# Layer 0 of a two-layer hybrid stack: where the modulation weights are fetched from, and how many places the gated z rows have

## The chip, the core and the metric

The kernel runs on one core of one Trainium2 chip. Its time is the device time of one execution in microseconds (us), taken from the host side of the program; the profile gives one execution's span, from its first instruction to its last. Five engines run their own instruction lists in order and wait for each other by semaphores: TensorE (PE), VectorE (DVE), ScalarE (ACT), GpSimd (POOL) and SyncE (SP). DMAs are issued by an engine's list too, and wait in it like any other instruction.

## The reference, cut to what matters

The program computes two blocks for 1024 tokens of 1024 channels. The first block has two layers, both modulated: from a vector `c`, `silu(c) @ ada_w[l] + ada_b[l]` gives a shift, a scale and a gate of 1024 each. Layer 0, the only part that the change touches, is this:

```
h    = rmsnorm(x) * (1 + scale) + shift
proj = h @ in_w                        # x half and z half, 1024 each
xf   = causal conv of 4 taps (x half)
r, i = sigmoid(block-diagonal gates of xf)
a    = exp(-8 * r * softplus(-lambda));  b = sqrt(1 - a^2) * (i * xf)
hseq = scan of  h_t = a_t * h_(t-1) + b_t
y    = hseq * silu(z half)
x    = x + gate * (y @ out_w)
```

Layer 1 (a gated delta rule) and the second block (convolution and state space) follow; the modulation of layer 1 needs its own columns of `ada_w`, and some of these are summed during layer 0.

## The kernel before, in words

Weights come as fp32 tiles `wst` of 1 MB over SP's queue (`load_w`, L101), and are split in two fp16 parts by ACT (`wh`, L104) and DVE (`wl`, L105), with two `wst` places and four places for the parts. A projection of 128 channels by 512 tokens is 24 matmuls (L111 to L113) into one of three PSUM places (`ps_mm`), which ACT empties: as `xp` for the x half (L323), as `silu` into `zs` for the z half (L542).

Layer 0 runs over four pairs of channel blocks. `xbranch(p)` projects the x half, makes the convolution (one ACT pass L329 and three DVE passes L331 for each of two halves e = 0 and 1), the gates (`ps_gate` matmuls L512, which wait for the L331 passes of their half, and ACT sigmoids L513), then decay and input on ACT and DVE (L519 to L528) and the scan (L531). `zbranch(p)` projects the z half in four groups; each goes through ACT L542 into a `zs` tile, is multiplied by `hseq` on DVE (L543), and split in two fp16 parts (ACT L123, DVE L125). There are two `zs` places.

Beside this run six sums of modulation columns, each over four tiles `ast` of 512 KB (24 tiles in all, four places). `ada_fetch` issues the four DMAs of one sum (L161), `ada_sum` makes eight DVE passes over them (L148 for the first, L150 for seven more), `ada_fin` transposes the sum on PE (L185), reduces and adds it on DVE (L186, L187) and writes 512 numbers to DRAM from POOL's queue (`ada_d`, L189). Each of these writes is a [128 x 4] tile of single fp32 numbers that go to scattered places of 4 bytes. The sums are called 1 to 6 here, and the tiles 1 to 24.

The order of instructions on each engine is not the order of the code: a list scheduler of the tile framework makes it, from dependences, places and its own estimate of times. So a change of a queue or of a number of places also moves instructions on engines that the diff doesn't name. Before the change POOL's list in this stage has little in it: clearing three columns of each `xp` (L313), and the six `ada_d` writes.

Of the kernel before, what the change touches and what calls it, by code (L numbers as in the profile page):

```python
# [10 lines left out]
F32 = mybir.dt.float32  # L11
# [6 lines left out]
P = 128  # L18
# [10 lines left out]
def kernel(ctx, tc, ins, out):  # L29
    nc = tc.nc  # L30
    pe, dve, act, pool, sp = nc.tensor, nc.vector, nc.scalar, nc.gpsimd, nc.sync
    a = ins

    def mkpool(name, bufs=1, space=None, stack=ctx):
        kw = {} if space is None else {"space": space}
        if space is not DRAM:
            kw["reuse_waits"] = "tile"
        return stack.enter_context(tc.tile_pool(name=name, bufs=bufs, **kw))
# [7 lines left out]
    def ps_mm(n="psmm"):  # L46
        return psmm.tile([P, 512], F32, tag="mm", name=n, bufs=3)
# [60 lines left out]
    def mm_chT(ps, w, c0, ah, al, nk=NK, ks=None):  # L108
        wh, wl = w
        for k in (range(nk) if ks is None else ks):  # L110
            pe.matmul(ps, wh[:, k, c0:c0 + P], ah(k), start=(k == 0), stop=False)  # L111
            pe.matmul(ps, wh[:, k, c0:c0 + P], al(k), start=False, stop=False)  # L112
            pe.matmul(ps, wl[:, k, c0:c0 + P], ah(k), start=False, stop=(k == nk - 1))  # L113
# [8 lines left out]
    def split(h, l, src, scale=1.0):  # L122
        act.activation(h, src, AF.Copy, scale=scale)  # L123
        if scale == 1.0:
            dve.tensor_tensor(out=l, in0=src, in1=h, op=ALU.subtract)  # L125
        else:
            dve.scalar_tensor_tensor(out=l, in0=src, scalar=scale, in1=h, op0=ALU.mult, op1=ALU.subtract)
# [24 lines left out]
    def ada_src(l, part, h, k0, n):  # L152
        c0 = D * part + 512 * h
        return a["ada_w"][l, P * k0:P * (k0 + n), c0:c0 + 512].rearrange("(k p) c -> p k c", p=P)

    def ada_fetch(pl, l, part, h):

        tiles = []
        for kk in range(4):
            st = pl.tile([P, 2, 512], F32, tag="ast", name="ast", bufs=4)  # L160
            sp.dma_start(st, ada_src(l, part, h, 2 * kk, 2))  # L161
            tiles.append(st)
        return tiles, l, part, h

# [74 lines left out]
    def hTh(sl):  # L239
        t = hT["h"]  # L240
        return lambda k: t[:, k, sl]

    def hTl(sl):
        t = hT["l"]
        return lambda k: t[:, k, sl]
# [88 lines left out]
    def shift_proj(w):  # L334
        wh, wl = w
        ps = ps_s("ps_sh")
        for e in range(2):
            es = slice(P * e, P * (e + 1))
            for k in range(NK):
                pe.matmul(ps[:, 2 * e:2 * e + 2], wh[:, k, es], shl[:, k, :], start=(k == 0), stop=False)  # L340
                pe.matmul(ps[:, 2 * e:2 * e + 1], wl[:, k, es], shl[:, k, 0:1], start=False, stop=(k == NK - 1))
        r = gwp.tile([P, 2, 2], F32, tag="shr", name="shr", bufs=3)
        act.activation(r.rearrange("p e t -> p (e t)"), ps[:, 0:4], AF.Copy, scale=IWS)
        dve.tensor_tensor(out=r[:, :, 0], in0=r[:, :, 0], in1=r[:, :, 1], op=ALU.add)
        return [r[:, e, 0:1] for e in range(2)]

    with ExitStack() as s0:
        pl = mkpool("ln0", stack=s0)
# [123 lines left out]
    with ExitStack() as sy:  # L472
        ypool = mkpool("y0", stack=sy)
        yT = []
        with ExitStack() as s0:
            pl = mkpool("lru", stack=s0)
# [57 lines left out]
            def zbranch(p, w):  # L534
                sb = shift_proj(w)
                for e in range(2):
                    yT.append([])
                    for hf in range(2):
                        ps = ps_mm()
                        mm_chT(ps, w, P * e, hTh(HF[hf]), hTl(HF[hf]))  # L540
                        zs = pl.tile([P, 512], F32, tag="zs", name="zs", bufs=2)
                        act.activation(zs, ps, AF.Silu, scale=IWS, bias=sb[e])  # L542
                        dve.tensor_tensor(out=zs, in0=zs, in1=hseq[p][:, e, HF[hf]], op=ALU.mult)  # L543

                        y = hseq[p][:, e, HF[hf]].bitcast(F16)
                        yT[-1].append((y[:, :512], y[:, 512:]))
                        split(y[:, :512], y[:, 512:], zs)

            adq = [(l, part, h) for l, part in ((0, 2), (1, 1), (1, 0)) for h in range(2)]
            adt, adp = [ada_fetch(pl, *adq.pop(0))], []  # L550

            def ada_step():
                if len(adp) == 2 or not adt:
                    ada_fin(pl, *adp.pop(0))
                if adt:
                    adp.append(ada_sum(pl, *adt.pop(0)))
                if adq:
                    adt.append(ada_fetch(pl, *adq.pop(0)))
# [5 lines left out]
            ada_step()  # L564
            wx.append(load_w(a["lru_in_w"][0], 3 * WC))
            zbranch(0, wz[0])
            ada_step()
            xbranch(2, wx[2])
            wz.append(load_w(a["lru_in_w"][0], D + 2 * WC))
            ada_step()  # L570
            zbranch(1, wz[1])
            wz.append(load_w(a["lru_in_w"][0], D + 3 * WC))
            ada_step()
            ada_step()
            xbranch(3, wx[3])
            ada_step()
            ada_step()
            zbranch(2, wz[2])
            ada_step()
            zbranch(3, wz[3])  # L580
        with ExitStack() as s0:
            pl = mkpool("out0", stack=s0)
# [29 lines left out]
    with ExitStack() as s0:  # L612
        pl = mkpool("gdn", stack=s0)
# [349 lines left out]
    with ExitStack() as s0:  # L963
        pl = mkpool("out1", stack=s0)
# [588 lines left out]
```

## Time and profile before

| | us |
|---|---|
| median of three runs | 1833.15 |
| lowest and highest | 1831.11, 1836.46 |
| the profiled execution, its time | 1828.97 |
| the profiled execution, its span | 1827.3 |
| PE busy | 1741.6 (95%) |
| DVE busy | 1386.6 (76%) |
| ACT busy | 920.1 (50%) |
| POOL busy | 62.1 (3%) |

PE is busy nearly everywhere, so what a change is worth is read from the stretches where it is not. Times are counted from the start of the span. Layer 0's four pairs run from about 80 to 273 us; everything later has the same order of instructions before and after.

### The profile page before, as it was taken

Reading aid. Unit: us, or ns where it says so; the run is one execution under the profiler, and the core shown is the slowest. Engines: PE = TensorE matmul, PEld = TensorE weight load, DVE = VectorE, ACT = ScalarE, POOL = GpSimd, SP = SyncE. Lnnn points to the kernel's source line nnn. Section 1 sums busy time; section 2 is a strip of 40 time slices with the busy share of each in tenths; the row PEclk is TensorE's granted clock in tenths of the full one; section 3 lists DMA queues with packets and bytes.
Section 4 is the critical chain, followed back from the end, with each engine's and each line's share of the span. In section 5 each row is a group of like instructions: output and inputs, shape, how many; then the busy total and the mean of one; then the engine's idle time right before and its main releaser. Section 6 shows DMA issues by size and latency. Waiting matters only on the chain.

```text
span 1827.3 us, 28998 instructions
## 1 busy us (share of the span) xinstructions
PE 1741.6 (95%) x11591; PEld 1072.6 (59%) x11591; DVE 1386.6 (76%) x2429; ACT 920.1 (50%) x1642; POOL 62.1 (3%) x152
## 2 busy tenths in 40 slices
PE   4978999999899999999999998999999999999998
PEld 2433449855556656678789586555444444444487
DVE  6697767656777777887466799999999999693332
ACT  6576663256556857766443434655651221571221
POOL 0000000000000010100000300000000000000000
PEclk8999999999999999999999999999999999999999
DMA  9554345314142231444342311101321221011212
GB/s 305 164 157 140 57 72 190 104 55 132 30 120 69 62 79 33 113 130 117 128 150 82 89 50 52 53 20 51 127 81 35 70 69 64 30 41 52 81 70 93
DMA packets 165169, 165.23 MB, mean 90 GB/s; under 512 B 50094, under 2 KB 143342, under 8 KB 165034
## 3 DMA queue, kind: packets, MB, share of 16 engines
q1 hardware_dynamic: 163626, 159.17, 29.0%
q0 software_dynamic: 1408, 4.21, 0.6%
q8 instruction: 91, 1.49, 0.3%
q14 instruction: 44, 0.36, 0.1%
HBM read 139.05 MB, written 23.12 MB: 89 GB/s over the span
## 4 chain that ended last, share of the span: by engine, by line
PE 61%; DVE 25%; ACT 6%; issue 4%; DMA 3%; SPq 0%; DVEq 0%; ACTq 0%
DVE cc L1024 5%; PE psmm L113 5%; PE psmm L111 5%; PE psmm L112 5%; DVE wl L105 2%; PE ps_out L120 2%; PE ps_out L118 2%; PE ps_out L119 2%; PE ps_fin L120 2%; PE ps_fin L118 2%; PE ps_fin L119 2%; PE ps_zc L111 2%; PE ps_zc L113 2%; PE ps_zc L112 2%; ACT jk L728 1%
## 5 line engine op out<-in xcount | busy, mean ns | idle before, releaser
L111 PE MATMUL psmm<-hTh,wh 128*128 128x512 f16 x896 | 342.2, 383 | 12.7 <-ACT zs L542 10.2
L112 PE MATMUL psmm<-hTl,wh 128*128 128x512 f16 x896 | 342.8, 383 | 0.1
L113 PE MATMUL psmm<-hTh,wl 128*128 128x512 f16 x896 | 342.8, 383 | 0.0
L1024 DVE SCALAR_TENSOR_TENSOR cc<-cu,cols,cc 128x1024 f32<-128x1024 f32 (+1 forms) x270 | 301.2, 1160 | 0.9
L112 PEld LDWEIGHTS <-wh 128*128 128x128 f16 x1568 | 154.2, 98 | 183.6 <-issue 18.7
L113 PEld LDWEIGHTS <-wl 128*128 128x128 f16 x1568 | 154.2, 98 | 175.0 <-issue 8.3
L111 PEld LDWEIGHTS <-wh 128*128 128x128 f16 x1568 | 154.2, 98 | 174.4 <-issue 8.2
L105 DVE SCALAR_TENSOR_TENSOR wl<-wst,wh 128x2048 f16<-128x2048 f32 (+2 forms) x71 | 153.6, 2168 | 51.7 <-ACT wh L104 51.7
L104 ACT ACTIVATE wh<-wst 128x2048 f16<-128x2048 f32 (+2 forms) x71 | 128.4, 1811 | 94.0 <-PE ps_gs L112 27.7
L118 PE MATMUL ps_z<-wh,hTh 128*128 128x256 f16 x256 | 69.8, 273 | 0.0
L120 PE MATMUL ps_z<-wl,hTh 128*128 128x256 f16 x256 | 69.8, 273 | 0.0
L119 PE MATMUL ps_z<-wh,hTl 128*128 128x256 f16 x256 | 69.8, 273 | 0.0
L118 PE MATMUL ps_fin<-wh,merged 128*128 128x256 f16 x256 | 69.8, 273 | 0.0
L119 PE MATMUL ps_fin<-wh,merged 128*128 128x256 f16 x256 | 69.8, 273 | 0.0
L120 PE MATMUL ps_fin<-wl,merged 128*128 128x256 f16 x256 | 69.8, 273 | 0.0
L119 PE MATMUL ps_out<-wh,hs 128*128 128x256 f16 x256 | 69.7, 273 | 0.0
L118 PE MATMUL ps_out<-wh,hs 128*128 128x256 f16 x256 | 69.7, 273 | 0.0
L120 PE MATMUL ps_out<-wl,hs 128*128 128x256 f16 x256 | 69.7, 273 | 0.0
L123 ACT ACTIVATE hTh<-ps_ht 128x512 f16<-128x512 f32 x32 | 17.4, 595 | 88.0 <-PE ps_ht L271 88.0
L793 DVE TENSOR_TENSOR Tt<-Tt,tm 128x60 f32<-128x60 f32 (+24 forms) x248 | 55.9, 225 | 5.5
L791 DVE TENSOR_TENSOR tm<-Lp,Tt 128x60 f32<-128x60 f32 (+24 forms) x248 | 53.6, 216 | 5.2
L120 PE MATMUL ps_out<-wl,yo 128*128 128x256 f16 x192 | 52.3, 273 | 0.3 <-DVE wl L105 0.3
(531 smaller groups left out, 3999.9 us busy)
## 6 DMA issues: line engine op xcount, KB each, us to landing
wst<-in_w_in_dram SPq DMA_DIRECT2D x24, 1024.0 KB
wst<-in_gdn_in_w_dram SPq DMA_DIRECT2D x16, 1024.0 KB
ast<-in_ada_w_dram SPq DMA_DIRECT2D x24, 512.0 KB
xt<-in_x_dram SPq DMA_DIRECT2D x16, 512.0 KB
wst<-in_lru_in_w_dram SPq DMA_DIRECT2D x8, 1024.0 KB
sta<-in_ada_w_dram SPq DMA_DIRECT2D x8, 1024.0 KB
wst<-in_lru_out_w_dram SPq DMA_DIRECT2D x4, 1024.0 KB
x_d<-xt POOLq DMA_DIRECT2D x8, 512.0 KB, 3.0
```

The costliest lines, as they stand in the source:

```text
L104: act.activation(hi, st, AF.Copy, scale=WS)
L105: dve.scalar_tensor_tensor(out=lo, in0=st, scalar=WS, in1=hi, op0=ALU.mult, op1=ALU.subtract)
L111: pe.matmul(ps, wh[:, k, c0:c0 + P], ah(k), start=(k == 0), stop=False)
L112: pe.matmul(ps, wh[:, k, c0:c0 + P], al(k), start=False, stop=False)
L113: pe.matmul(ps, wl[:, k, c0:c0 + P], ah(k), start=False, stop=(k == nk - 1))
L118: pe.matmul(ps, ah(k), wh[:, k, :], start=(k == 0), stop=False)
L119: pe.matmul(ps, al(k), wh[:, k, :], start=False, stop=False)
L120: pe.matmul(ps, ah(k), wl[:, k, :], start=False, stop=(k == nk - 1))
L728: act.activation(jk, pst[:, P * c:P * (c + 1)], AF.Square, accum_out=kq[:, n, 4 * b + c:4 * b + c + 1])
L791: dve.tensor_tensor(out=tv, in0=Lp[:, j, j + 1:].unsqueeze(1).to_broadcast([P, m, n]), in1=Tt[:, :m, j:j + 1].to_broadcast([P, m, n]), op= ...
L793: dve.tensor_tensor(out=Tt[:, :m, j + 1:], in0=Tt[:, :m, j + 1:], in1=tv, op=ALU.subtract)
L1024: dve.scalar_tensor_tensor(out=acc, in0=cus[j][:, i + t0:i + t0 + n], scalar=col("cw", j, i), in1=acc, op0=ALU.mult, op1=ALU.add)
```

## The change

```diff
@@ ada_fetch
             st = pl.tile([P, 2, 512], F32, tag="ast", name="ast", bufs=4)
-            sp.dma_start(st, ada_src(l, part, h, 2 * kk, 2))
+            pool.dma_start(st, ada_src(l, part, h, 2 * kk, 2))
@@ zbranch
-                        zs = pl.tile([P, 512], F32, tag="zs", name="zs", bufs=2)
+                        zs = pl.tile([P, 512], F32, tag="zs", name="zs", bufs=4)
```

All 24 `ast` DMAs leave SP's list for POOL's, and `zs` gets four places. The scheduler then makes another order for layer 0. Three places of it:

POOL, from its first instructions to the end of layer 0 (`xp` is a memset, `ast` a load, `ada_d` a write of one finished sum):

```order
-L313 MEMSET xp 128x3 x4
-L189 DMA ada_d<-adac 128x4x1 x2
+L313 MEMSET xp 128x3 x2
+L161 DMA ast<-in_ada_w_dram 128x2x512 x12
+L313 MEMSET xp 128x3 x2
+L189 DMA ada_d<-adac 128x4x1
+L161 DMA ast<-in_ada_w_dram 128x2x512 x4
 L313 MEMSET xp 128x3
-L189 DMA ada_d<-adac 128x4x1 x4
+L189 DMA ada_d<-adac 128x4x1
+L161 DMA ast<-in_ada_w_dram 128x2x512
+L189 DMA ada_d<-adac 128x4x1
+L161 DMA ast<-in_ada_w_dram 128x2x512 x7
+L189 DMA ada_d<-adac 128x4x1 x3
```

Tile 17 now stands right behind the second write, and tile 18 right behind the third.

DVE, between the gates of pair 1 and its decay (`gt` are gate values, `at` the decay):

```order
-L148 TENSOR_SCALAR ad<-ast,ccol 128x512
-L150 SCALAR_TENSOR_TENSOR ad<-ast,ccol,ad 128x512 x5
-L186 TENSOR_REDUCE adac<-ps_ada 128x4
-L150 SCALAR_TENSOR_TENSOR ad<-ast,ccol,ad 128x512
+L150 SCALAR_TENSOR_TENSOR ad<-ast,ccol,ad 128x512 x7
 L523 TENSOR_TENSOR gt_901<-gt_901,xf 128x2048
-L150 SCALAR_TENSOR_TENSOR ad<-ast,ccol,ad 128x512
-L187 TENSOR_TENSOR adac<-adac,cols 128x4
-L148 TENSOR_SCALAR ad<-ast,ccol 128x512
 L524 SCALAR_TENSOR_TENSOR gt_888<-gt_888,at 128x2048
 L543 TENSOR_TENSOR zs<-zs,hs 128x512 x2
-L150 SCALAR_TENSOR_TENSOR ad<-ast,ccol,ad 128x512 x6
 L527 SCALAR_TENSOR_TENSOR at<-gt_888,at 128x2048
```

The passes over `ast` tiles that stood between L523 and L527 are gone from there.

DVE, ahead of the first convolution passes (L331) of the last pair; before the change:

```order
L187 TENSOR_TENSOR adac<-adac,cols 128x4
L150 SCALAR_TENSOR_TENSOR ad<-ast,ccol,ad 128x512
L344 TENSOR_TENSOR shr<-shr 128x2
L105 SCALAR_TENSOR_TENSOR wl<-wst,wh 128x2048
L150 SCALAR_TENSOR_TENSOR ad<-ast,ccol,ad 128x512 x2
L331 SCALAR_TENSOR_TENSOR xf<-xp,cols,xf 128x1024
```

and with it:

```order
L187 TENSOR_TENSOR adac<-adac,cols 128x4
L150 SCALAR_TENSOR_TENSOR ad<-ast,ccol,ad 128x512
L186 TENSOR_REDUCE adac<-ps_ada 128x4
L150 SCALAR_TENSOR_TENSOR ad<-ast,ccol,ad 128x512
L187 TENSOR_TENSOR adac<-adac,cols 128x4
L344 TENSOR_TENSOR shr<-shr 128x2
L150 SCALAR_TENSOR_TENSOR ad<-ast,ccol,ad 128x512
L105 SCALAR_TENSOR_TENSOR wl<-wst,wh 128x2048
L150 SCALAR_TENSOR_TENSOR ad<-ast,ccol,ad 128x512
L148 TENSOR_SCALAR ad<-ast,ccol 128x512
L150 SCALAR_TENSOR_TENSOR ad<-ast,ccol,ad 128x512 x6
L331 SCALAR_TENSOR_TENSOR xf<-xp,cols,xf 128x1024
```

Eight more passes over `ast` tiles and one more L186 stand ahead of L331, among them the first over tile 17 (the L148) and over tile 18 (within the last six).

## Rows read from the trace of the kernel before

**Rows 1.** Windows: stretch, us, busy PE, PEld, DVE, ACT, POOL, PEclk, DMA share, GB/s.

```profile
185.00:230.00 45.00, 45.00 (x262) 21.80 (x261) 36.58 (x37) 31.10 (x34) 1.50 (x2) 1.00 0.36 72
```

**Rows 2.** Timeline of PE: start, us, instruction, count, [idle before, releaser].

```profile
123.70 7.14 PE L512 MATMUL ps_gate<-xf,gw 128*128 128x512 f32 x12 [2.64 <-DVE xf L331]
130.67 0.60 PE L185 MATMUL ps_ada<-ident,ad 128*128 128x128 f32 x4
137.87 0.58 PE L111 MATMUL psmm<-hTh,wh 128*128 128x512 f16 x1 [6.60 <-ACT zs L542]
...
154.04 0.38 PE L111 MATMUL psmm<-hTh,wh 128*128 128x512 f16 x1 [3.63 <-ACT zs L542]
...
171.25 1.13 PE L512 MATMUL ps_gate<-xf,gw 128*128 128x512 f32 x2 [1.50 <-DVE xf L331]
```

**Rows 3.** Timeline of ACT, pair 1.

```profile
108.55 1.91 ACT L526 ACTIVATE at<-at 128x2048 f32<-128x2048 f32 x1
...
137.13 1.26 ACT L542 ACTIVATE zs<-psmm,shr 128x512 f32<-128x512 f32 x2
143.70 2.00 ACT L525 ACTIVATE gt<-gt,onecol 128x2048 f32<-128x2048 f32 x1 [5.30 <-DVE gt L524]
...
153.31 0.69 ACT L542 ACTIVATE zs<-psmm,shr 128x512 f32<-128x512 f32 x1 [0.20 <-DVE hs L125]
```

**Rows 4.** Timeline of DVE, pair 1.

```profile
111.20 2.29 DVE L527 SCALAR_TENSOR_TENSOR at<-gt,at 128x2048 f32<-128x2048 f32 x1
...
140.98 0.48 DVE L148 TENSOR_SCALAR ad<-ast,ccol 128x512 f32<-128x512 f32 x1 [4.20 <-DMA ast<-in_ada_w_dram]
...
144.79 3.52 DVE L150 SCALAR_TENSOR_TENSOR ad<-ast,ccol,ad 128x512 f32<-128x512 f32 x5
```

**Rows 5.** Chain that ended last, around pair 1: start, us, what.

```profile
125.74 7.26 DMA ast<-in_ada_w_dram
...
136.74 12.89 DMA ast<-in_ada_w_dram
```

**Rows 6.** Windows of 1 us, same columns; the last is GB/s.

```profile
81.00:82.00 1.00, 1.00 (x9) 0.58 (x8) 0.61 (x8) 0.21 (x1) 0.00 (x0) 1.00 1.09 388
...
133.00:134.00 1.00, 0.00 (x0) 0.00 (x0) 0.91 (x2) 0.99 (x2) 0.00 (x0) 1.00 0.64 39
...
217.00:218.00 1.00, 1.00 (x6) 0.49 (x5) 1.00 (x2) 0.00 (x0) 0.00 (x0) 1.00 1.00 39
```

**Rows 7.** Timeline of POOL: a cleared `xp`, and two of the six writes.

```profile
75.40 0.10 POOL L313 MEMSET xp<- 128x3 f32 x1 [5.01 <-DVE adac L389]
...
126.09 0.97 POOL L189 DMA_DIRECT2D ada_d<-adac  x1 [2.20 <-DVE adac L187]
...
211.51 0.75 POOL L189 DMA_DIRECT2D ada_d<-adac  x1 [40.07 <-DVE adac L187]
```

**Rows 8.** POOL's DMAs by line: first `x_d` (L593), then `ada_d` (issue, landing).

```profile
DMA to landing us min/median/max: 2.9/3.0/5.9
...
L189 POOL DMA_DIRECT2D ada_d<-adac x8: 750/754/969, 126.1 to 709.1; - x8
...
DMA to landing us min/median/max: 8.3/9.6/12.4
```

**Rows 9.** Timelines of SP and ACT: weight loads of layer 0, and a weight split.

```profile
77.58 2.57 SPq L101 DMA_DIRECT2D wst<-in_lru_in_w_dram  x2
...
83.21 1.90 ACT L104 ACTIVATE wh<-wst 128x2048 f16<-128x2048 f32 x1
```

**Rows 10.** Timelines of DVE and PE, last pair.

```profile
208.87 0.68 DVE L543 TENSOR_TENSOR zs<-zs,hs 128x512 f32<-128x512 f32 x1
...
211.87 2.28 DVE L105 SCALAR_TENSOR_TENSOR wl<-wst,wh 128x2048 f16<-128x2048 f32 x1
...
215.52 1.28 DVE L331 SCALAR_TENSOR_TENSOR xf<-xp,cols,xf 128x1024 f32<-128x1024 f32 x1
...
220.90 1.88 PE L512 MATMUL ps_gate<-xf,gw 128*128 128x512 f32 x4
```

## The prediction

> **What bounds the kernel now.** I read the page's busy shares first (PE 95%, so a gain can only come out of the few stretches where PE waits), then PE's timeline through layer 0, then, for each gap in it, the engine that the gap names, and last the DMA windows. PE's gaps between 120 and 172 us are four [rows 2]: 2.64 us before the gates of pair 1 (waiting for a DVE convolution pass), 6.60 and 3.63 us before projections (waiting for ACT to empty a PSUM place through `zs`), and 1.50 us before the gates of pair 2. From 185 to 230 us PE is busy for 45.00 of 45 us [rows 1]. So what this stage can give is some 14 us (2.64 + 6.60 + 3.63 + 1.50), and after it PE's own work sets the time.
>
> Behind two of the gaps stands an `ast` load. DVE stood for 4.20 us at the L148 of a tile that had not landed [rows 4]; behind it in DVE's list was L524, for which ACT's L525 stood 5.30 us [rows 3]; and behind L525 in ACT's list stands the L542 at 153.31 that PE's 3.63 us waited for [rows 2, 3]. The loads that came late took 7.26 and 12.89 us from issue to use [rows 5]. They were issued at 125.74 and 136.74, beside the first two `ada_d` writes (one of them at 126.09 [rows 7]). Such a write takes 8.3 to 12.4 us to land, though it is 2 KB, against a median of 3.0 us for an `x_d` store of 512 KB [rows 8]; and while one is on its way the whole core's DMA falls from 388 GB/s to 39, here at 133 us and again at 217 us, 7 and 6 us after a write [rows 6, 7].
>
> **Part 1, loads off SP's list and the passes regrouped: pair 1.** With the loads on POOL, tiles 1 to 12 are issued with no `ada_d` ahead of them, and the scheduler has put all passes of sum 3 ahead of L523, none between L523 and L527. DVE then reaches L524 without a load to wait for. Three terms:
> - Before the gates of pair 1, DVE's L527 started at 111.20, 0.74 us after ACT's L526 had ended (108.55 + 1.91) [rows 3, 4], since passes over `ast` were in its way. One of them now stands earlier, so L527 starts when ACT allows: 0.7 us off, and all that follows on ACT and DVE moves with it.
> - The 6.60 us stay: PE waits there for an L542 (137.13) that stands behind ACT's sigmoids, which have not become shorter.
> - ACT's L525 follows its two L542 (137.13 + 1.26 = 138.4) at once instead of at 143.70. From L525's start to the end of the next L542 it is 9.6 + 0.7 = 10.3 us [rows 3], and part of that was a weight split that now stands behind. So the PSUM place is free by 148.7; PE would want it at 154.04 - 3.63 = 150.4. The 3.63 us go. The chain to the L331 passes of pair 2 moves by about as much, and PE arrives last: the 1.50 us go too.
>
> Sum 0.7 + 3.6 + 1.5 = **5.8 us gained by 172 us**.
>
> **Part 2, four `zs` places.** At 153.31 ACT waited 0.20 us for a place [rows 3]; the other waits of this kind are as small. That is all that two more places give directly. What they do is let two L542 stand together in the order, and that is in part 1 already.
>
> **Part 3, what the loads collide with at the start.** The last `xp` memset ahead of them ran at 75.40 [rows 7], so tiles 1 to 4 (2.1 MB) go out from 75.5, ahead of the two `wst` loads that SP issued from 77.58 [rows 9]; before, they were behind those. ACT's L104 ran at 83.21 [rows 9], on the first of these. At 388 GB/s [rows 6] the four tiles need 5.4 us; started at about 76.5 they have some 1 MB left when the weights are at full rate, near 80. If the weights get half of the engines until then, the first lands 2 us later; if none, 2.6 us; if tiles 1 to 4 are quicker than I think, nothing. Some of this is slack, as L104 did not wait for its load before. I take 1.4 us, with bounds of 0 and 2.6; L104 stands in ACT's list ahead of the convolution and gates of the first pairs, so I let it pass on to everything up to the last pair. The Trainium skill (DMA: Bandwidth & Descriptors, section Queues, rings and completion order) says that a DMA engine takes turns between queues, a packet at a time; by it the half share holds and the term would be 2 us less the slack, the same place in the range. No run so far shows two full queues at once.
>
> Later collisions are covered. POOL's `xp` memsets stand behind twelve loads now, but their readers come tens of us later. SP's weight loads no longer stand behind `ast` waits; I count nothing for that, as PE's gaps name no weight.
>
> **Part 4, the last pair: where it is given back.** Here the order puts eight more passes over `ast` tiles and one more L186 ahead of the first L331. Take the L543 at 208.87 [rows 10] as mark. It moves to 208.9 - 5.8 + 1.4 = 204.5.
> - DVE's way to tile 17. Before, L105 came 3.0 us after the mark. Now L186 (0.7 by its neighbours' size) and two L150 (0.69 each, the pace of five in 3.52 us [rows 4]) are added, 5.1; L105 with 2.2 and one more L150 follow, 8.0. DVE stands at tile 17's L148 at 212.5.
> - Tile 17's landing. Write 2 was issued 2.64 us after the mark in the order before (211.51 [rows 7]); DVE's steps up to it are the same, so it goes out at 207.1, and tile 17 behind it at 207.9 (0.75 us of issue [rows 8]). Landing: between a clean 3.0 us [rows 8] and the 7.26 and 12.89 us of a load beside a write [rows 5]. It is issued as close behind a write as those two were, so I take these: 215.2 to 220.8. **DVE stands 2.7 to 8.3 us.**
> - Tile 18 stands behind write 3, some 1.7 us later, and lands some 1.7 us later; DVE reaches it 2.4 us later. No more is lost if it too takes 7 to 13 us.
> - Then L148 and six L150 (4.6) and the three L331 with two L150 between (4.9): the last pair's first gates can start at 212.5 + 2.7 to 8.3 + 9.5 = 224.7 to 230.3.
> - PE would be there at 220.90 - 4.4 = 216.5, plus what the order now puts ahead of these gates: eight transposes (0.15 each [rows 2]) and five projection matmuls (0.22 each: 72 of them from 154.04 to 169.75 [rows 2]), 2.3 us: 218.8. **PE waits 5.9 to 11.5 us.**
>
> Between the gates of the two halves DVE and PE then need about as long as each other, and PE's work after it is the same less what was moved ahead, so this wait is not caught up.
>
> **Sum.** -5.8 + 1.4 + (5.9 to 11.5, middle 8.7) = +1.5 to +7.1, middle **+4.3 us**. Against the profiled execution's own 1828.97 that is 1833.3. That execution was 4.2 us under the median of the runs, 1833.15, so I put the change on the median: **1837.4 us**, +0.23%. The uncertain start (0 to 2.6 for 1.4) widens this case to 0 to +8.3.
>
> **The rivals.**
> *Clean landing.* Tiles 17 and 18 take 3.0 us like `x_d` and DVE never stands. For it: the slow stretch comes some us after a write's issue, and a load that follows quickly may slip through; one load lands in 3 us if alone. Against it: both loads of [rows 5] were issued as close. DVE is then through its L331 at 212.5 + 9.5 = 222.0, PE still waits 3.2 us for the eight passes, and the sum is -5.8 + 1.4 + 3.2 = -1.2: 1832.0. The Trainium skill (same page, section Anatomy of one DMA) gives a DMA from GpSimd's queue as 2.0 us plus its bytes at 436 GB/s: an estimate of 3.2 us for a 512 KB tile. The `x_d` rows agree with it, the `ast` rows beside a write don't.
> *One ring, in order: slower.* Writes 2 and 3 and tiles 17 and 18 now share POOL's queue. If write 3's small pieces start only when tile 17 is through, its own slow stretch of some 8 us comes after tile 17's landing and falls whole on tile 18: 218 + 8 to 11 = 226 to 229, first gates 7 us later, PE's wait 14 to 17, the sum +10 to +13: 1843 to 1846. It decides if the two slow stretches follow each other instead of overlapping. For it: the same queue. Against: a DMA engine that is through with its share of tile 17 can begin with write 3 at once, so that the stretches should overlap in part.
> *Nothing given back.* DVE has time enough (the passes fit where it stood idle) and PE is not held at the last pair: -4.4, with an undisturbed start -5.8: 1827.4 to 1828.8. Against it: the order has the eight passes ahead of L331, and PE is there by 218.8.
>
> **Chances.** Forecast 0.5, clean 0.2, one ring 0.2, nothing given back 0.1. A measurement of this kernel can tell about 0.3% (5.5 us) from no change. Faster than that only at the end of the last rival: 0.04. Slower: one ring, 0.2, and the upper third of the forecast, 0.14. Within: 0.62. The range of 8 in 10 leaves out the last rival and the upper half of the ring: 1831 to 1844.5.
>
> **What would show it.** After the change: DVE idle before an L148 or L150 behind a DMA near 212 to 223 us (2.7 to 8.3 us), and PE idle before the last pair's first gates (6 to 11 us) that was not there; no 4.20 us before L148 and no 3.63 us before the projection in pair 1; L104 a little after 83.21. If DVE's stop is missing the clean rival holds; if PE's gap is over 13 us, the ring. It would be wrong altogether if the start cost more than 3 us, or if layer 0's later order holds a wait that I haven't seen.

## The result, and the profile after

The change made the kernel slower: 1855.34 us (median, 1853.38 to 1858.73) against 1832.13, a ratio of 1.0128 with a 95% interval of 1.011 to 1.0145. The prediction was 1837.4 with 1831.0 to 1844.5; the sign of its sum was right, its size was not. The profiled execution's span is 1851.2 us, 23.9 more than before. PE's idle time grew by 12.2 us and its busy time by 11.7 (1753.3 against 1741.6), with the same matmuls (11591 in both): so half of the loss is matmuls that took longer, at a mean granted clock of 0.979 for 0.989.

Where it went is read from lags: the start of an instruction after the change, less its start before. It is +6.75 us at pair 1's first projection that waits (144.62 for 137.87), +1.26 at the gates of pair 2 (172.51 for 171.25), +19.93 at the last `x_d` store of layer 0 (383.46 for 363.53), and some 23 from 530 us on. So three stretches matter: the start loses, pair 1 gives most of that back, and from there to the end of layer 0 the last pair loses 18.7 (19.93 - 1.26).

**The start.** Windows of the change (columns as in [rows 1]), then timelines of POOL, SP, ACT and PE, and PE's first gates in the kernel before:

```profile
76.00:78.00 2.00, 2.00 (x11) 0.76 (x9) 2.00 (x2) 0.00 (x0) 1.99 (x3) 1.00 0.35 37
78.00:80.00 2.00, 2.00 (x11) 0.70 (x9) 1.66 (x1) 0.01 (x1) 1.00 (x2) 1.00 0.88 320
80.00:82.00 2.00, 2.00 (x12) 0.86 (x11) 0.70 (x8) 0.79 (x2) 0.00 (x0) 1.00 1.03 386
```

```profile
75.88 3.11 POOL L161 DMA_DIRECT2D ast<-in_ada_w_dram  x4 [0.47 <-issue]
...
77.49 2.57 SPq L101 DMA_DIRECT2D wst<-in_lru_in_w_dram  x2
...
86.82 1.91 ACT L104 ACTIVATE wh<-wst 128x2048 f16<-128x2048 f32 x1 [3.60 <-DMA wst<-in_lru_in_w_dram]
...
90.91 0.16 PE L340 MATMUL ps_sh<-shl,wh 128*128 128x2 f16 x1 [2.42 <-ACT shr L343]
...
92.72 5.17 PE L512 MATMUL ps_gate<-xf,gw 128*128 128x512 f32 x6 [1.22 <-DMA gw<-in_lru_gate_w_dram]
```

```profile
88.87 2.82 PE L512 MATMUL ps_gate<-xf,gw 128*128 128x512 f32 x6
```

The L104 of [rows 9], which had not waited, now stands 3.60 us for its weights. PE waits for the shift matmuls behind it (small ones, of the weights with the modulation's shift), then for `gw`, the gates' weights, which SP issues behind the two `wst` loads; and the six gate matmuls then take 5.17 us for 2.82 before.

**Pair 1.** Timelines of DVE, ACT and PE (the places of [rows 2 to 4]):

```profile
142.61 2.29 DVE L524 SCALAR_TENSOR_TENSOR gt<-gt,at 128x2048 f32<-128x2048 f32 x1 [1.21 <-ACT gt L522]
...
145.04 2.00 ACT L525 ACTIVATE gt<-gt,onecol 128x2048 f32<-128x2048 f32 x1
...
144.62 0.59 PE L111 MATMUL psmm<-hTh,wh 128*128 128x512 f16 x1 [6.28 <-ACT zs L542]
...
172.51 1.88 PE L512 MATMUL ps_gate<-xf,gw 128*128 128x512 f32 x4
```

DVE's 4.20 us and ACT's 5.30 us of [rows 3, 4] are gone, and with them PE's 3.63 and 1.50 us: 6.75 - 1.26 = 5.5 us come back.

**The last pair.** Timelines of POOL, DVE and PE; then windows from the gates of pair 2 to the last `x_d` store, the kernel before and the change, and one of the stretch with the stops:

```profile
213.61 0.78 POOL L189 DMA_DIRECT2D ada_d<-adac  x1 [44.43 <-DVE adac L187]
214.37 0.71 POOL L161 DMA_DIRECT2D ast<-in_ada_w_dram  x1
215.61 0.78 POOL L189 DMA_DIRECT2D ada_d<-adac  x1 [0.53 <-DVE shr L344]
216.38 0.71 POOL L161 DMA_DIRECT2D ast<-in_ada_w_dram  x1
...
226.79 0.49 DVE L148 TENSOR_SCALAR ad<-ast,ccol 128x512 f32<-128x512 f32 x1 [7.88 <-DMA ast<-in_ada_w_dram]
...
232.67 2.08 DVE L150 SCALAR_TENSOR_TENSOR ad<-ast,ccol,ad 128x512 f32<-128x512 f32 x3 [3.41 <-DMA ast<-in_ada_w_dram]
...
212.29 0.16 PE L340 MATMUL ps_sh<-shl,wh 128*128 128x2 f16 x1 [2.87 <-DVE adac L186]
...
234.23 1.08 PE L185 MATMUL ps_ada<-ident,ad 128*128 128x128 f32 x4 [6.13 <-DVE ad L150]
...
240.98 3.59 PE L512 MATMUL ps_gate<-xf,gw 128*128 128x512 f32 x4 [3.53 <-DVE xf L331]
```

```profile
171.25:363.53 192.28, 192.28 (x1357) 129.46 (x1358) 135.71 (x169) 100.66 (x125) 9.33 (x18) 1.00 0.39 103
```

```profile
172.51:383.46 210.95, 197.96 (x1362) 131.29 (x1361) 141.46 (x179) 101.39 (x124) 16.19 (x27) 0.97 0.37 103
230.00:275.00 45.00, 37.24 (x204) 18.04 (x205) 34.21 (x36) 28.11 (x31) 4.42 (x6) 0.89 0.44 134
```

The core's DMA in this stretch, in slices of 1 us from 205 to 245 us:

```profile
GB/s 0 0 0 0 0 0 0 0 0 0 14 61 12 25 41 33 16 12 16 45 337 341 117 176 134 152 151 114 190 352 428 341 401 377 270 57 74 279 172 82
```

After write 2 at 213.61 us it is slow for ten slices (12 to 61 GB/s), then fast for two, in which tile 17 comes in, then slower again for seven (114 to 190 GB/s), in which write 3 and tile 18 are on their way. Write 2 lands 9.2 us after its issue, write 3 16.4 us after. Tile 17 is used 12.4 us after its issue, tile 18 16.3 us after. PE stands 2.87 + 6.13 + 3.53 = 12.5 us. After such a stop it runs at the lower of its two levels: the four gate matmuls at 240.98 take 3.59 us for 1.88 [rows 10], the four transposes 1.08 for 0.60 [rows 2]; the granted clock, 1.00 in [rows 1], is 0.89 from 230 to 275 us. From the gates of pair 2 to the last `x_d` store PE is busy for 5.7 us more (197.96 for 192.28): with 12.5 us and a stop of 0.46 us at 182 us that is the whole 18.7.

One more view tells what was moved. Windows of the tile `ad` alone, first before, then after (columns PE, PEld and DVE busy; DVE's count is the number of passes):

```profile
100.00:172.00 72.00, 1.23 (x8) 0.92 (x8) 16.57 (x24) 0.93 0.47 138
172.00:300.00 128.00, 2.24 (x16) 1.94 (x16) 11.40 (x16) 1.00 0.43 102
```

```profile
100.00:172.00 72.00, 0.63 (x4) 0.42 (x4) 10.27 (x15) 0.91 0.40 95
172.00:300.00 128.00, 3.32 (x20) 2.65 (x20) 16.66 (x24) 0.95 0.36 87
```

A whole sum, eight passes, left pair 1 for the last pair (24 passes after 172 us for 16).

### The profile page after: what moved, and what is told of

It reads as the page before. It is cut to its first block, busy times and chain, and to the rows that moved or that the text cites. A ratio compares the mean times of both kernels' runs of the same rounds, so it can differ in the third digit from the quotient of the medians.

```text
span 1851.2 us, 29005 instructions
## 1 busy us (share of the span) xinstructions
PE 1753.3 (95%) x11591; PEld 1077.8 (58%) x11591; DVE 1387.4 (75%) x2429; ACT 919.9 (50%) x1641; POOL 80.1 (4%) x176
## 4 chain that ended last, share of the span: by engine, by line
PE 57%; DVE 25%; ACT 7%; issue 7%; DMA 3%; SPq 0%; POOL 0%; DVEq 0%; ACTq 0%; POOLq 0%
DVE cc L1024 5%; PE psmm L113 4%; PE psmm L111 4%; PE psmm L112 4%; DVE wl L105 3%; PE ps_out L120 2%; PE ps_out L118 2%; PE ps_out L119 2%; PE ps_fin L118 2%; PE ps_fin L119 2%; PE ps_fin L120 2%; PE ps_zc L113 1%; PE ps_zc L112 1%; PE ps_zc L111 1%; PE ps_gate L512 1%
## 5 line engine op out<-in xcount | busy, mean ns | idle before, releaser
L112 PEld LDWEIGHTS <-wh 128*128 128x128 f16 x1568 | 154.6, 99 | 180.8 <-issue 16.4
L104 ACT ACTIVATE wh<-wst 128x2048 f16<-128x2048 f32 (+2 forms) x71 | 128.4, 1812 | 96.1 <-PE ps_gs L112 27.7
```

The costliest lines, as they stand in the source:

```text
L104: act.activation(hi, st, AF.Copy, scale=WS)
```

## The experiments

Ratios are against the kernel before on the same chip. "Lag" is that of the last `x_d` store of layer 0, from the profiles; "passes" those over `ast` tiles after 172 us.

| run | median us | ratio, 95% | lag | passes |
|---|---|---|---|---|
| the change | 1855.34 | 1.0128, 1.011 to 1.0145 | +19.9 | 24 |
| e1_pool_only | 1855.03 | 1.0134, 1.0119 to 1.0149 | +22.4 | 24 |
| e2_zs4_only | 1830.65 | 0.9997, 0.9982 to 1.0012 | -1.1 | 16 |
| e3_first_on_sp | 1836.40 | 1.0025, 1.0013 to 1.0038 | +2.8 | 16 |
| e4_16byte_write | 1842.51 | 1.0063, 1.0043 to 1.0084 | +7.3 | 24 |
| e5_write_on_sp | 1851.20 | 1.0108, 1.0078 to 1.0139 | +22.3 | 24 |
| e9_first_on_pool | 1836.92 | 1.0031, 1.0019 to 1.0043 | +6.3 | 16 |
| e10_late_start | 1836.55 | 1.0032, 1.0019 to 1.0045 | +5.1 | 17 |
| e12_16byte_before | 1827.45 | 0.9977, 0.9966 to 0.9988 | -4.9 | 16 |
| f1_sum_after_pair | 1857.34 | 1.0132, 1.0113 to 1.0152 | +22.7 | 24 |
| g1_sum_after_16byte | 1847.01 | 1.0081, 1.0055 to 1.0106 | +12.7 | 24 |
| f4_late_16byte | 1832.83 | 0.9998, 0.9987 to 1.001 | -3.6 | 16 |
| f2_16byte_right | 1827.94 | 0.9971, 0.9957 to 0.9986 | -5.5 | 16 |
| f3_16byte_early_bias | 1827.26 | 0.9972, 0.996 to 0.9984 | -2.6 | 16 |

**The two halves of the change.** e1 is the change without its second line, e2 the kernel before with it:

```diff
-                        zs = pl.tile([P, 512], F32, tag="zs", name="zs", bufs=2)
+                        zs = pl.tile([P, 512], F32, tag="zs", name="zs", bufs=4)
```

> The change without its second part: all 24 ast loads from GpSimd's queue, but two zs places. The lists of PE, DVE, POOL and SP are word for word those of the change; only ACT's differs, at three places around L542. Theory (the queue of the loads makes the new order, the collision at the start and the late tiles; the zs places do nothing): 1855 us, within 4 us of the change, the same 3.6 us wait of L104 near 87 us and the same stop of DVE of some 8 us near 227 us. Rival (the two additional zs places let ACT run its L542 in twos, and that moved the order): well under 1850 us.

> The second part alone: four zs places, ast loads on SP's queue as before. The lists of PE, DVE, POOL and SP are those of the kernel before; ACT has two L542 together at a few places. Theory (a zs place cost 0.2 us of waiting at the gap that mattered): 1832 us, within 2 us of before. Rival (two L542 together free a PSUM place earlier and the 3.63 us gap goes even with the loads on SP): 1826 to 1829.

All of the loss is the queue of the loads; the `zs` places do nothing. The scheduler makes the change's order on DVE and PE from the queue alone.

**Tiles 1 to 4 back on SP.**

```diff
-            pool.dma_start(st, ada_src(l, part, h, 2 * kk, 2))
+            (sp if (l, part, h) == (0, 2, 0) else pool).dma_start(st, ada_src(l, part, h, 2 * kk, 2))
```

> The change with tiles 1 to 4 (the first fetch alone) back on SP's queue; tiles 5 to 24 stay on GpSimd's, four zs places. The scheduler then gives PE and DVE nearly the order of the kernel before (10 and 11 lines of difference in the whole program): the eight additional passes ahead of the last pair's L331 are gone, though the loads still share a queue with the ada_d writes. Theory A (the loss is the collision at the start plus the order ahead of the last pair, which comes from where the scheduler believes tiles 1 to 4 to be): L104 runs at 83 us without a wait, PE's gaps at 212 to 241 us are gone, 1829 to 1838 us. Theory B (the loss is the queue that loads and writes share, whatever the order): DVE still stands some 8 us for a tile behind a write at a place that PE waits for, 1845 us or more. The kernel before is 1832, the change 1855.

Theory A holds: 1836.40 us. Twenty loads share a queue with the writes, and in this order the kernel is only some 5 us longer (1831.23 before). DVE still stands for a tile behind a write, now in pair 1, and PE's gap there, 3.63 us in the kernel before, is 5.85 (timelines of ACT, DVE and PE):

```profile
82.10 1.90 ACT L104 ACTIVATE wh<-wst 128x2048 f16<-128x2048 f32 x1
...
144.03 0.49 DVE L148 TENSOR_SCALAR ad<-ast,ccol 128x512 f32<-128x512 f32 x1 [9.34 <-DMA ast<-in_ada_w_dram]
...
155.06 0.58 PE L111 MATMUL psmm<-hTh,wh 128*128 128x512 f16 x1 [5.85 <-ACT zs L542]
```

**The pieces of a write.** Four neighbouring numbers per partition, in the change and in the kernel before:

```diff
-        pool.dma_start(ada_d[l, c0:c0 + 512].rearrange("(k p) -> p k", p=P), o)
+        pool.dma_start(ada_d[l, c0:c0 + 512].rearrange("(p k) -> p k", p=P), o)
```

> The change with each ada_d write as 128 pieces of 16 bytes (four neighbours of one partition) in place of 512 pieces of 4 bytes; every engine's list is as in the change. What is left out: the numbers of a sum land in another order within their 512, so the shift, scale and gate rows made from them belong to other channels. Theory (the number of small pieces makes the slow stretch in which the core's DMA falls to 40 GB/s): a write lands in 3 to 5 us in place of 8 to 12, tiles 17 and 18 land 3 to 6 us after issue, DVE's stop of 7.9 us before L148 near 227 us shrinks to 2 or less, and of the loss some 10 to 16 us come back: 1839 to 1845. The collision at the start and the eight passes stay. Rival (a load behind a write in one queue is late whatever the write's pieces are): DVE still stands 6 us or more, 1851 to 1856.

> The kernel before with its ada_d writes as 128 pieces of 16 bytes; every list as before. What is left out: the numbers of a sum land in another order within their 512, as in the 16-byte run of the change. Theory (the slow stretch behind the writes made the 7.26 and 12.89 us loads of pair 1): DVE's stop of 4.20 us before L148 at 141 us goes to under 1 us, PE's 3.63 us before the projection and some of the 1.50 us go, 1826 to 1829. Rival (those loads are late for another reason, their place in SP's list): the 4.20 us stay and 1830 to 1833.

Issue to landing of the eight writes, min/median/max: the change, then the same with 16-byte pieces; and DVE and PE of the latter at the last pair:

```profile
DMA to landing us min/median/max: 8.2/9.3/16.4
```

```profile
DMA to landing us min/median/max: 1.7/2.2/4.8
```

```profile
217.93 0.49 DVE L148 TENSOR_SCALAR ad<-ast,ccol 128x512 f32<-128x512 f32 x1 [0.15 <-DMA ast<-in_ada_w_dram]
...
211.16 0.16 PE L340 MATMUL ps_sh<-shl,wh 128*128 128x2 f16 x1 [2.88 <-DVE adac L186]
...
229.93 1.98 PE L512 MATMUL ps_gate<-xf,gw 128*128 128x512 f32 x4 [1.45 <-DVE xf L331]
```

With every list unchanged, a write of the same 2 KB lands four times sooner, DVE's 7.88 us go to 0.15, PE's 12.5 us to 4.3, and 19.9 - 7.3 = 12.6 us of lag come back. In the kernel before the same edit takes 3.7 us off: DVE's 4.20 us and PE's 3.63 and 1.50 us are not in that trace. So the slow stretch that the prediction found in [rows 6 to 8] is made by the scattered 4-byte pieces; whether by their number (512 for 128) or by their size, the edit, which changes both, doesn't tell.

**The queue of a write.** Still 4-byte pieces:

```diff
-        pool.dma_start(ada_d[l, c0:c0 + 512].rearrange("(k p) -> p k", p=P), o)
+        sp.dma_start(ada_d[l, c0:c0 + 512].rearrange("(k p) -> p k", p=P), o)
```

> The change with the eight ada_d writes moved from GpSimd's queue to SP's, still 512 pieces of 4 bytes each; the lists of PE, DVE and ACT are word for word those of the change, the loads stay on GpSimd's. Theory (the slow stretch is the write's own, on the core's 16 DMA engines, whatever queue it is in): tiles 17 and 18 are issued about a microsecond earlier, but land late all the same, DVE still stands 6 to 8 us for tile 17, 1850 to 1857. Rival (the loads are late because they stand behind the write in one queue): DVE's stop goes to 2 us or less, 1838 to 1845 as with the 16-byte pieces.

```profile
213.87 2.36 SPq L189 DMA_DIRECT2D ada_d<-adac  x2
...
214.80 0.72 POOL L161 DMA_DIRECT2D ast<-in_ada_w_dram  x1 [45.13 <-DVE ad L150]
...
227.57 0.49 DVE L148 TENSOR_SCALAR ad<-ast,ccol 128x512 f32<-128x512 f32 x1 [8.14 <-DMA ast<-in_ada_w_dram]
```

(SP's queue, POOL and DVE.) Tile 17 has a queue without a write in it and is as late, 12.8 us from issue to use. The theory holds: a tile is late without a write ahead of it in its queue. Both writes still share one queue here, SP's, and tile 18 is late too.

**The start by itself.** The kernel before with only tiles 1 to 4 from GpSimd:

```diff
-            sp.dma_start(st, ada_src(l, part, h, 2 * kk, 2))
+            (pool if (l, part, h) == (0, 2, 0) else sp).dma_start(st, ada_src(l, part, h, 2 * kk, 2))
```

> The kernel before with only tiles 1 to 4 taken from GpSimd's queue; tiles 5 to 24 stay on SP's, two zs places. The collision at the start by itself: in the order, pair 1 is changed a little on DVE (72 lines), and the passes ahead of the last pair's L331 are fewer, not more. Theory (the collision costs about 6 us on the way into pair 1's gates): L104 of the first pair waits 3 to 4 us for its weights and runs near 87 us, the gates of pair 1 come 5 to 6 us later, and what of it is left at the end depends on pair 1's waits: 1832 to 1838. Rival (the late L104 came from the whole of the change's order): L104 at 83 to 84 us without a wait, 1828 to 1832.

```profile
76.47 3.11 POOL L161 DMA_DIRECT2D ast<-in_ada_w_dram  x4 [0.48 <-issue]
...
87.53 1.91 ACT L104 ACTIVATE wh<-wst 128x2048 f16<-128x2048 f32 x1 [3.72 <-DMA wst<-in_lru_in_w_dram]
```

The collision makes L104 wait 3.7 us without the rest of the change, and this kernel ends 5.8 us later. Its order in pair 1 differs from that of before too, so not all of the 5.8 us need be the collision. And the other way round, the change with tiles 1 to 4 held back:

```diff
-            st = pl.tile([P, 2, 512], F32, tag="ast", name="ast", bufs=4)
+            st = pl.tile([P, 2, 512], F32, tag="ast", name="ast", bufs=4); (l, part, h) == (0, 2, 0) and pool.tensor_copy(st[:, 0, 0:1], gw[1][:, 0:1])
```

> The change with tiles 1 to 4 held back: GpSimd copies one column of gw into each tile ahead of its load, so that the loads start when the gates' weights have landed, near 90 us, and don't run beside the first weight loads. The scheduler then puts the eight additional passes of the last pair behind its L331 again. Theory (collision at the start plus order ahead of the last pair): L104 at 83 us without a wait, no PE gap over 3 us near 212 to 241 us, 1829 to 1838. Rival (any load that shares the queue with a write costs PE at the last pair): 1845 or more.

It lands in the range (1836.55), but with a gap that the theory hadn't: DVE stands 7.97 us for a tile behind a write, and PE before pair 2's gates (DVE, PE):

```profile
139.92 0.75 DVE L150 SCALAR_TENSOR_TENSOR ad<-ast,ccol,ad 128x512 f32<-128x512 f32 x1 [7.97 <-DMA ast<-in_ada_w_dram]
...
173.05 3.78 PE L512 MATMUL ps_gate<-xf,gw 128*128 128x512 f32 x4 [5.63 <-DVE xf L331]
```

**The order of the last pair: a theory that fell.** The change with one of the two `ada_step()` ahead of `xbranch(3)` moved behind it:

```diff
-            ada_step()
             xbranch(3, wx[3])
+            ada_step()
```

> The change with one of the two sums that the code finishes ahead of the last pair moved behind the last pair's xbranch. Every list is that of the change up to the last pair; from there the passes over tiles 17 and 18 stand behind the first L331 passes, as in the kernel before. The collision at the start stays. Theory (the order of the last pair plus late tiles is some 18 us of the 23): DVE runs the last pair's L105 and L331 without a wait for a tile, PE has no gap over 3 us from 212 to 241 us but the 2.9 us before its shift matmuls; what is left is the collision less pair 1's gain, 1833 to 1840. Rival (the time is lost behind the writes wherever the passes stand, as DVE reaches tiles 17 and 18 some us later and waits then): 1848 or more.

> The run with the sum moved behind the last pair's xbranch, and the writes in 16-byte pieces (the numbers of a sum land in another order within their 512). Every list as in that run, which took 1857 us with DVE standing 8.30 us for a tile at 243 us and PE 7.33, 4.30 and 2.99 us. Theory L (a late tile is what costs, wherever the order puts its passes; the one sum more that is left for the last pair costs little when its tiles come in time): DVE's stop under 2 us, 1834 to 1841, at or under the 1842.5 us of the change with 16-byte pieces. Theory S (one sum more in the last pair costs by its work, eight passes, eight transposes and their order, on time or not): 1847 or more.

f1 (POOL, DVE, PE), and g1 (DVE, PE, a window with all columns):

```profile
228.58 0.77 POOL L189 DMA_DIRECT2D ada_d<-adac  x1 [3.32 <-DVE adac L187]
231.03 0.71 POOL L161 DMA_DIRECT2D ast<-in_ada_w_dram  x1 [1.68 <-DVE ad L150]
...
242.93 0.49 DVE L148 TENSOR_SCALAR ad<-ast,ccol 128x512 f32<-128x512 f32 x1 [8.30 <-DMA ast<-in_ada_w_dram]
...
247.12 1.09 PE L185 MATMUL ps_ada<-ident,ad 128*128 128x128 f32 x4 [7.33 <-DVE ad L150]
...
261.86 1.09 PE L185 MATMUL ps_ada<-ident,ad 128*128 128x128 f32 x4 [4.30 <-DVE ad L150]
```

```profile
236.41 0.49 DVE L148 TENSOR_SCALAR ad<-ast,ccol 128x512 f32<-128x512 f32 x1 [1.56 <-DMA ast<-in_ada_w_dram]
...
251.84 1.09 PE L185 MATMUL ps_ada<-ident,ad 128*128 128x128 f32 x4 [2.47 <-DVE ad L150]
256.74 0.59 PE L111 MATMUL psmm<-hTh,wh 128*128 128x512 f16 x1 [2.98 <-ACT zs L542]
```

```profile
250.00:260.00 10.00, 5.18 (x44) 2.96 (x45) 7.79 (x11) 8.37 (x9) 1.13 (x2) 0.58 0.28 107
```

In f1 the gap at 212 us and the first gates' wait are gone, as I expected, and nothing is saved: the next late tile (behind write 3) meets DVE ahead of L523, and PE waits by its transposes L185 and then for ACT. In g1 the tiles are nearly in time and 10 us come back, but PE still stops 2.47 and 2.98 us, and the clock is 0.58 in the window that holds both. From the gates of pair 2 to the end of layer 0 the lag grows by 18.7 us in the change, 7.2 in e4, 21.2 in f1 and 10.9 in g1. So theories L and S both hold in part: late tiles cost 10 to 11.5 us, and what is left, 7 to 11 us with the tiles nearly in time, goes with the one sum more in the last pair. Where the passes stand within the last pair decided little here.

**Both causes mended, and a faster kernel.** f4 is e10 with 16-byte writes. f2 and f3 are the kernel before with 16-byte writes whose numbers are in their own places, which they are not in e4, e12 and g1: the transposes take every fourth column, and the biases are loaded in that order. The edit, without the loads of the biases:

```diff
-            pe.transpose(pst[:, P * kk:P * (kk + 1)], acc[:, P * kk:P * (kk + 1)], ident)
+            pe.transpose(pst[:, P * kk:P * (kk + 1)], acc.rearrange("p (c k) -> p k c", k=4)[:, kk], ident)
...
-        pool.dma_start(ada_d[l, c0:c0 + 512].rearrange("(k p) -> p k", p=P), o)
+        pool.dma_start(ada_d[l, c0:c0 + 512].rearrange("(p k) -> p k", k=4), o)
```

> The change mended in both places: tiles 1 to 4 held back until gw has landed, and the writes in 16-byte pieces with the right result (biases loaded early). Order as in the run with tiles 1 to 4 held back. That run had DVE 7.97 us at an L150 at 140 us and PE 5.63 us before the gates of pair 2, behind a write; theory: both go, 1828 to 1831, near the kernel before. If the queue itself cost something beyond the two causes: 1834 or more.

> The kernel before with 16-byte pieces and the right result: the transposes take every fourth column, so that a partition holds four neighbouring numbers, and the biases come in that order over GpSimd's queue, held back until the gates' weights have landed. PE, DVE, ACT and SP have the order of before. If strided transposes and two loads of biases cost nothing, the same as the 16-byte run of before with its numbers in the wrong places: 1827 to 1829, ratio 0.998. If the loads of biases (1024 pieces of 16 bytes near 90 us) make a slow stretch of their own on the way to tiles 1 to 4: 1829 to 1833.

> As the run with 16-byte pieces and the right result, but the biases are loaded near the start of the program. The same order otherwise. If the 1024 pieces are slow beside the first loads of x and of ada_w, 1829 or more; if not, 1827 to 1828.

f4 is level with the kernel before (0.9998; its median of 1832.83 lies between the two expectations): with both causes mended the loss of the change is gone. It doesn't follow that the queue of the loads costs nothing. f2 and f3, with the same writes and the loads on SP's queue, are 0.29% and 0.28% faster than the kernel before, and f4 is 4.9 and 5.6 us longer than they are; the executions of the three scatter by 2.0 to 2.6 us (standard deviation, 10 to 12 of each), so that difference is clear of noise. The profiles show 1.8 us of it by the end of layer 0 against f2 and none against f3 (lags -3.6, -5.5 and -2.6); where the rest lies wasn't found. The two loads of biases (4.8 and 5.5 us to landing in f2) don't show in the times at either place (1827.94 and 1827.26; 1827.45 in e12 without them).

## Why the prediction was wrong, step by step

**Part 1 held in each of its terms, not in their sum.** The 0.7 us is in the lag, which falls from 6.20 us at the second gates of pair 0 (98.60 for 92.40) to 5.48 at pair 1's gates (129.18 for 123.70). The 3.63 and 1.50 us are gone: the lag falls by 5.5 us from 144.62 to 172.51, and e12 takes the same two PE gaps away by another cause, the write. But between these two stretches 1.3 us are lost that the sum didn't have: the twelve gate matmuls of pair 1 take 8.4 us for 7.14, at a granted clock of 0.65 for 0.76. So 4.9 us came back for 5.8. One reading was loose: the tile that DVE stood 4.20 us for is neither of the two in [rows 5] but tile 13, issued at 128.19 and used at 140.98, 12.8 us, which is inside the bounds taken from those two.

**Part 2 was right**: e1 and e2 show the `zs` places to be worth nothing that can be measured.

**Part 3 was mis-sized**: +6.20 us at 98.60 us for +1.4 (bounds 0 to 2.6). The prediction had named this as a sign that it would be wrong altogether, a start that costs more than 3 us. Two steps failed. The first is what the four tiles took from the weights' loads. I had some 1 MB of the tiles left near 80 us, and half of the engines for the weights until they were through. The windows give 37 GB/s for 2 us and 320 GB/s for 2 us, some 0.7 MB, moved by 80 us, so 1.4 MB of the 2.1 were left. What each queue moved from then on can be read (packets, MB, share of the engines; q0 is GpSimd's queue, q1 is SP's): in the change from 80 to 86 us, and in the kernel before from 76 to 82 us.

```profile
q0 software_dynamic: 382, 1.38, 56.9%
q1 hardware_dynamic: 982, 1.00, 47.2%
```

```profile
q1 hardware_dynamic: 1001, 1.02, 52.3%
```

The rest of the tiles and the first MB of weights came in side by side, the weights with 42% of the bytes (1.00 of 2.38 MB); that MB was in at 86 us, where the kernel before had it at 82. Of these 4 us L104 had a little slack to give, and it waited 3.60. The half share was my own step from the rule of the Trainium skill (DMA: Bandwidth & Descriptors, Queues, rings and completion order) that a DMA engine takes turns between queues, a packet at a time. The trace agrees that both queues move at once; as the profile counts packets it has 982 of one for 382 of the other, so equal turns of these are not what it shows. The second step is that I followed L104 alone: PE stopped for the shift matmuls (2.42 us) and for `gw` (1.22), and the first six gate matmuls took 2.35 us longer, 6.0 us together.

**Part 4 had the place and the mechanism, and half of the price**: +18.7 us for +8.7 (5.9 to 11.5). Tile 17's landing (12.4 for 7.26 to 12.89) and DVE's stop (7.88 for 2.7 to 8.3) were inside my bounds. (The write at 211.51 that I took for write 2 in the order before is the third there; its place behind the mark, 2.64 us, is what counted, and it was 2.66.) Three steps failed. "No more is lost" at tile 18 stood on a landing of 7 to 13 us: it took 16.3 us, in the second slow stretch, and DVE stood 3.41 us more, and 1.17 at a later tile. I priced only the gates as PE's wait; they had 3.53 us, and PE also waited for the sum's transposes (L185, 6.13) and the shift matmuls behind L186 (2.87), 12.5 us together. And the sum had no term for the clock: PE was busy for 45 of 45 us in [rows 1], and I took its matmuls' durations as given when PE would stop; they doubled for a while after each stop, which was 5.7 us.

**The rivals.** Clean landing and nothing given back were wrong. One ring, in order, came nearest: 10 to 13 us over before, and a PE gap over 13 us as its sign, where PE stood 12.5. It said that write 3's slow stretch comes after tile 17's landing and falls on tile 18, and the trace has that: two slow stretches with a fast one between them, write 3 and tile 18 landing at 232.0 and 232.6 us. My argument against it, that the stretches should overlap, failed. Whether the shared queue is what puts them in a row is not shown: in e5 the writes share SP's queue instead, and tile 17 is as late and tile 18 later (12.8 and 17.3 us from issue to use). Its size was short of the 23 us because the start and the clock were not in it either. The Trainium skill (DMA: Bandwidth & Descriptors, Issuing engines are not separate DMA queues) says that the DMAs of all engines run on the same 16 DMA engines and interleave; the trace agrees, with 12.8 us for tile 17 in e5, where the write is in another queue, for 12.4. The Trainium skill (DMA: Bandwidth & Descriptors, Rules for kernel authors) says that a last dimension which isn't contiguous becomes one descriptor per element; the row that bears on it is the landing of the writes, 9.3 us, and 2.2 with four numbers in a piece. I had the row of 8.3 to 12.4 us [rows 8] and did not ask what made it.

**After layer 0** the lag grows by another 3.4 us in this profile, with equal lists. Such drifts come without the change too: f2, whose lists of PE, DVE, ACT and SP are those of before, goes from -5.3 us at 376 us to -1.1 at 920, and e3 from +2.8 to +1.4. So these 3.4 us need not be a cost of the change. The profiled execution of before lay 4.2 us under its median. What differs from execution to execution there wasn't tried.

**What stays open**: the collision and the additional sum are not separable in the change's own order, since any edit at the start moves the passes (e3, e10). How much of the last pair's 7 us in e4 is the sum's work and how much its order, no run tells. And why f4 is some 5 us behind f2 and f3, with loads on GpSimd's queue and neither of the two causes left, is open.

## What to carry to other kernels

A stall that a reordering removes early has to be looked for later: count the moved work by stage (passes, loads) on both sides, since here the eight passes that left pair 1 stood in the last pair's way. A store whose pieces are a few bytes is to be costed as a slow stretch for the core's loads, those in other queues too (e5), and cured at the store. Where PE was never idle, price a new stop at more than its length: here 12.5 us of stops came with 5.7 us of slower matmuls. And compare a mended change with the kernel before mended in the same way: f4 looks level beside the kernel before, and is 5 us behind f2.

## What was not expected of the hardware

- A write of 2 KB in 512 pieces of 4 bytes takes 8.2 to 16.4 us from issue to landing in the change; in 128 pieces of 16 bytes it takes 1.7 to 4.8 us in e4, and 6.3 at most in the other runs.
- Four loads of 512 KB, issued 1.6 us ahead of two loads of weights in another queue, left these 42% of the bytes for six microseconds, and the first MB of weights came 4 us later.
- Stops of PE of 12.5 us in all at the last pair came with 5.7 us of slower matmuls: a granted clock of 0.89 from 230 to 275 us, where it had been 1.00.
